# Expert rows built in two parts and a hand-written VectorE order between mixer and experts

## The chip, the cores and the metric

The kernel runs on one core of one Trainium2 chip. The time is device microseconds of one execution. Engines are named as in the profile: PE is TensorE, DVE is VectorE, ACT is ScalarE, POOL is GpSimd, SP is SyncE (it only issues transfers here).

## The reference

Two layers over 1024 tokens of width 1024, in float32. Layer 0 mixes with sliding-window attention, layer 1 with a diagonal state-space scan and a gated output projection (GLU). After each mixer comes a mixture of 32 experts:

```python
x = x + g1 * mix
h = rms_norm(x, norm_ffn[layer]) * (1.0 + sc2) + sh2
x = x + g2 * hierarchical_moe(h, ...)      # weights of this layer
```

The expert stage takes the softmax over 4 groups, the best group, and in it the two best of 8 experts. Each token goes to two experts, each `silu(x Wg) * (x Wu)` times `Wd` with 256 hidden columns, and the two results are added by their gates.

## The kernel before

Tokens stand in 8 row tiles of 128. Every float32 product is made of three products of a high and a low part; the low part of a weight tile comes from DVE (L939), the high part from ACT (L938). A layer runs in four steps: the mixer, its last projection, the handoff, and the experts.

The last projection runs in units. In layer 0 a unit is one row tile and one half of the columns (16 units, row by row). In layer 1 it is one row tile and a quarter of the columns (32 units, column by column, tile `x2`). Work of the routing is placed between the matmuls of a unit: `late(k)` takes the squares and transposes of unit k-1, and `early(k)` the logits of unit k-2. PE's order is the order of the code. DVE's order is chosen by a scheduler.

Once a row tile has all its logits, `scale` makes its `rms` by thirteen small dependent DVE operations (L720 to L118), and `rows_out` writes the expert row `h = (x * rms) * scr + shr` with two operations, L729 and L730, and sends it from POOL to `hrow` in DRAM. In layer 0 this is done in place in the residual's tile `xr`, which is also being stored to `xmid`. In layer 1 the row goes to a tile `hr` of two buffers.

Rows are routed in groups 0-2, 3-5 and 6-7 (`route`, tiles `r00`, `r03`, `r06` in layer 0 and `r10`, `r13`, `r16` in layer 1). A route finds the two experts of each token (L754 to L770), adds them to the running counts `seen` (L776), and lets PE make the positions within each expert (`lp`, L781/782, two `yield`s later). One step later the one-hot slots `so` (L803) let PE add the group to the lists in `lst` (L808). `drain` finishes what is left after the last unit.

`moe_lists` turns `lst` into the gather's indices `ligi` (L866, L867), the scatter's indices and gates, and `cnt` into the number of overflow blocks `nov`. `moe` then gathers rows for the first four experts into `xg` (L929), and PE transposes them (`e_0pt`, L949). Weight tiles come through the rotating tiles `w`, `pair` and `ring` on SP's queue. A load into a tile waits until the tile's last reader has ended, for a `w` tile often the low-part split L939. In layer 0 the experts run beside preparation for layer 1, which loads the tiles `b`.

## Time and profile before

| What | us |
|---|---|
| Median of 3 runs (lowest, highest) | 1846.93 (1841.4, 1850.45) |
| The profiled execution | 1847.04 |
| Its span, first to last instruction | 1845.3 |
| Output projection of layer 0, about | 366 to 500 |
| First handoff | 500 to 535 |
| Experts of layer 0 | 535 to about 880 |
| GLU projection of layer 1 | 1236 to 1438 |
| Second handoff | 1438 to 1473 |
| Experts of layer 1 | 1473 to 1800 |

Over the span PE is busy 84% and DVE 68%. Such shares are means over stages with different limits; what the change is worth is read in the two handoffs and in the units before them. A busy PE need not run at its full clock: the column PEclk gives the granted clock as a share of 2.4 GHz.

### The profile page before, as it was taken

How to read it: one execution, taken by the hardware profiler on the slowest of the kernel's cores; microseconds unless marked ns; L12 is line 12 of the kernel's file. 1: busy time of each engine (PE TensorE's matmuls, PEld its weight loads, DVE VectorE, ACT ScalarE, POOL GpSimd, SP SyncE). 2: the span in 40 equal slices, each digit the busy share in tenths (PEclk: the TensorE clock that was granted, in tenths of full speed). 3: DMA queues.
4: the chain of work that ended last, by engine and by line, in shares of the span. 5: the costliest groups of instructions: out<-in, count | busy, mean ns of one | idle time of the engine just before them, and what ended most of it. 6: DMA issues, size and time to landing. Idle time of an engine off the chain costs nothing. (4 is left out here: it accounts for less than half of the span.)

```text
span 1845.3 us, 20788 instructions
## 1 busy us (share of the span) xinstructions
PE 1559.1 (84%) x6935; PEld 1118.4 (61%) x6935; DVE 1247.4 (68%) x2311; ACT 748.9 (41%) x1455; POOL 438.2 (24%) x385
## 2 busy tenths in 40 slices
PE   4799969899849998999889677769999499999991
PEld 1576624377637665666467565648887377777760
DVE  4886779766567986766455699862216677777764
ACT  3211137621135554555311366532222165565640
POOL 1410014421112121111000577532220212222210
PEclk8799989999969999899999888889999599999995
DMA  9656750053449899989274011331002589999937
GB/s 364 216 212 245 294 151 1 15 206 120 172 164 355 303 330 327 318 324 318 94 257 149 25 37 40 97 124 46 33 18 88 214 320 348 381 388 374 360 124 281
DMA packets 124997, 379.85 MB, mean 206 GB/s; under 512 B 44908, under 2 KB 63428, under 8 KB 94168
## 3 DMA queue, kind: packets, MB, share of 16 engines
q1 hardware_dynamic: 94648, 301.89, 45.4%
q0 software_dynamic: 23040, 50.37, 7.2%
q10 hardware_dynamic: 7200, 26.22, 3.8%
q8 instruction: 57, 0.93, 0.2%
q14 instruction: 52, 0.43, 0.1%
HBM read 355.43 MB, written 56.53 MB: 223 GB/s over the span
## 5 line engine op out<-in xcount | busy, mean ns | idle before, releaser
L1742 PE MATMUL gpo<-gh,yh 128*128 128x512 f32 x256 | 106.7, 417 | 9.8 <-ACT gh L1717 9.8
L1742 PE MATMUL gpo<-gl,yh 128*128 128x512 f32 x256 | 101.5, 397 | 1.7 <-POOL gl L1718 1.7
L1742 PE MATMUL gpo<-gh,yl 128*128 128x512 f32 x256 | 101.4, 396 | 0.0
L929 POOL DMA_INDIRECT xg<-hrow,ligi x64 | 80.3, 1255 | 53.0 <-issue 14.9
L222 DVE SCALAR_TENSOR_TENSOR acc<-w,cs,acc 128x2048 f32<-128x2048 f32 x35 | 83.5, 2387 | 6.0 <-DMA w<-in_w_ada 5.6
L1748 DVE SCALAR_TENSOR_TENSOR gth<-gth,gpo 128x256 f32<-128x256 f32 x32 | 13.4, 419 | 107.4 <-ACT gth L1747 107.4
L1742 PEld LDWEIGHTS gpo<-gh,yh 128*128 128x128 f32 x256 | 49.2, 192 | 18.3 <-ACT gh L1717 10.1
L624 PE MATMUL wopo<-woh,a_hi 128*128 128x512 f32 x128 | 55.2, 431 | 1.6 <-ACT woh L598 1.6
L1742 PEld LDWEIGHTS gpo<-gl,yh 128*128 128x128 f32 x256 | 49.1, 192 | 10.5 <-POOL gl L1718 2.2
L1742 PEld LDWEIGHTS gpo<-gh,yl 128*128 128x128 f32 x256 | 48.8, 191 | 10.5
L624 PE MATMUL wopo<-wol,a_hi 128*128 128x512 f32 x128 | 52.7, 412 | 2.7 <-POOL wol L599 2.7
L1650 PE MATMUL bpo<-wih,bhh 128*128 128x512 f32 x128 | 52.0, 407 | 1.8 <-ACT bhh L1640 1.8
L624 PE MATMUL wopo<-woh,a_lo 128*128 128x512 f32 x128 | 52.3, 408 | 0.0
L1650 PE MATMUL bpo<-wil,bhh 128*128 128x512 f32 x128 | 50.9, 398 | 0.0
L1650 PE MATMUL bpo<-wih,bhl 128*128 128x512 f32 x128 | 50.1, 400 | 0.3 <-DVE bhl L1641 0.2
L1750 POOL TENSOR_TENSOR gth<-gth,g 128x256 f32<-128x256 f32 x24 | 17.5, 730 | 110.0 <-DVE gth L1748 110.0
L624 PEld LDWEIGHTS wopo<-wol,a_hi 128*128 128x128 f32 x128 | 25.4, 198 | 8.4 <-POOL wol L599 3.8
L1652 DVE SCALAR_TENSOR_TENSOR u<-bpo,n_y,shw 128x512 f32<-128x512 f32 x16 | 12.0, 750 | 26.4 <-PE bpo L1650 26.4
L1650 PEld LDWEIGHTS bpo<-wih,bhh 128*128 128x128 f32 x128 | 24.3, 190 | 8.9 <-ACT bhh L1640 3.7
L624 PEld LDWEIGHTS wopo<-woh,a_hi 128*128 128x128 f32 x128 | 25.1, 196 | 7.2 <-ACT woh L598 2.5
L624 PEld LDWEIGHTS wopo<-woh,a_lo 128*128 128x128 f32 x128 | 25.2, 197 | 6.0
L1650 PEld LDWEIGHTS bpo<-wih,bhl 128*128 128x128 f32 x128 | 24.2, 189 | 7.5 <-DVE bhl L1641 1.7
(2707 smaller groups left out, 4857.2 us busy)
## 6 DMA issues: line engine op xcount, KB each, us to landing
ring<-in_moe_w_down SPq DMA_DIRECT2D x64, 1024.0 KB
w<-in_w_ada SPq DMA_DIRECT2D x48, 1024.0 KB
w<-in_moe_w_gate SPq DMA_DIRECT2D x32, 1024.0 KB
w<-in_moe_w_up SPq DMA_DIRECT2D x32, 1024.0 KB
pair<-in_moe_w_gate SPq DMA_DIRECT2D x32, 1024.0 KB
pair<-in_moe_w_up SPq DMA_DIRECT2D x32, 1024.0 KB
w<-in_ssm_w_glu SPq DMA_DIRECT2D x16, 512.0 KB
w<-in_attn_w_qkv SPq DMA_DIRECT2D x6, 1024.0 KB
```

Of the source, the lines that this page charges most:

```text
L222: eng.scalar_tensor_tensor(acc, w, self.cs[:, j:j + 1], acc, op0=ALU.mult, op1=ALU.add)
L624: T.matmul(po, a[:, kk, j], w[:, j, :], start=(i == 0), stop=(i == 23))
L929: G.indirect_dma_start(out=self.xg, out_offset=None, in_=me.hrow[l], in_offset=bass.IndirectOffsetOnAxis(ap=self.gcol, axis=0), bounds_che ...
L1650: T.matmul(po, a[:, 4 * hf + j, :], w[:, j, :], start=(k == 0), stop=(k == 23))
L1652: V.scalar_tensor_tensor(u[:, 32 * c:32 * c + 32, 7 - i, :], po.rearrange("p (g c) -> p g c", c=16), r, self.shw[:, 512 * c:512 * c + 512] ...
L1742: T.matmul(po, a[:, 2 * q + j, :], w[:, j, :], start=(n == 0), stop=(n == 23))
L1748: V.scalar_tensor_tensor(th, th, 1.0, po[:, 0], op0=ALU.add, op1=ALU.mult)
L1750: E.tensor_tensor(th, th, g1[:, cs], op=ALU.mult)
```

## The change

An expert row is now made in two parts. `rows_in` makes `x * scr`, by halves in layer 0 and before `rms` is known, into a tile `hr` of its own (one buffer in layer 0, two in layer 1). `rows_out` makes `h * rms + shr` with one operation. In layer 0 the residual's tile `xr` has two buffers instead of three. Rows 6 and 7 are scaled one by one in both layers, the last row is written after its route, and `route` has one `yield` less. `drain` runs with DVE's order fixed as written, and `settle` advances the open routes. The weight splits of the first expert, the counts and `nov` are issued behind the copy `routed`. The pools of `moe` are opened in another order, so that `mw` (the split weight tiles) and the new `mx` (tiles `xh`, `xl`) lie elsewhere.

```diff
@@ mixer_a
-        units, early, late, drain = self.moe_front(0, 2, lambda nm: xp.tile([P, D], F32, name=nm, tag="xr", bufs=3))
+        units, early, late, settle, drain = self.moe_front(0, 2)
-                    xts[m] = xp.tile([P, D], F32, name=f"xr{m}", tag="xr", bufs=3)
+                    xts[m] = xp.tile([P, D], F32, name=f"xr{m}", tag="xr")
@@ moe_front
-        gain = rowtile(f"gain2{l}")
+        gain = fp.tile([P, D], F32, name=f"gain2{l}", tag="hr", bufs=1 + l)
...
+        def rows_in(m, lo, hi):
+            if m not in hs:
+                hs[m] = fp.tile([P, D], F32, name=f"f{l}{m}hr", tag="hr", bufs=1 + l)
+            V.tensor_tensor(hs[m][:, lo:hi], xs[m][:, lo:hi], scr[:, lo:hi], op=ALU.mult)
         def rows_out(m):
-            h = rowtile(f"f{l}{m}hr") if l else xs[m]
-            V.scalar_tensor_tensor(h, xs[m], rms[:, m:m + 1], scr, op0=ALU.mult, op1=ALU.mult)
-            V.tensor_tensor(h, h, shr, op=ALU.add)
+            if m not in hs:
+                rows_in(m, 0, D)
+            h = hs[m]
+            V.scalar_tensor_tensor(h, h, rms[:, m:m + 1], shr, op0=ALU.mult, op1=ALU.add)
             G.dma_start(hrows[:, m], h)
@@ route, before lp
             yield
-            yield
@@ route
-            S.activation(ex, ex, AF.Exp)
+            self.last_exp = S.activation(ex, ex, AF.Exp)
@@ late
                 hts[k - 1] = squares(m, xs[m], c)
+                if l == 0 or (c == parts - 1 and m >= GROUPS[-2]):
+                    rows_in(m, width * c, width * c + width)
+            if l and 0 <= k < len(units) and units[k][0] >= GROUPS[-2] and units[k][1] == parts - 1:
+                m = units[k][0]
+                xs[m] = tile_of(m)
+                rows_in(m, 0, D - width)
+        def finished(k):
+            if not 0 <= k < len(units):
+                return None
+            m, c = units[k]
+            logits(m, c, hts.pop(k))
+            if c < parts - 1 or m + 1 not in GROUPS:
+                if c == parts - 1 and (l == 0 or m >= GROUPS[-2]):
+                    scale(m, m + 1)
+                    rows_out(m)
+                return None
+            m0 = GROUPS[GROUPS.index(m + 1) - 1]
+            if l and m0 < GROUPS[-2]:
+                scale(m0, m + 1)
+                for i in range(m0, m + 1):
+                    rows_out(i)
+            else:
+                scale(m, m + 1)
+                if m + 1 < NT:
+                    rows_out(m)
+            return route(m0, m + 1)
         def early(k):
...
+            r = finished(k - 2)
+            settle()
+            if r:
+                next(r)
+                running.append(r)
+        def settle():
+            for r in list(running):
                 if next(r, True):
                     running.remove(r)
         def drain(tile_of):
             k = len(units)
-            early(k)
-            late(k, tile_of)
-            early(k + 1)
-            while running:
-                k += 1
-                early(k + 1)
+            with self.tc.manual_schedule(engines={ET.DVE}):
+                late(k, tile_of)
+                finished(k - 2)
+                settle()
+                last = finished(k - 1)
+                for _ in last:
+                    pass
+                rows_out(NT - 1)
@@ moe_lists (cnt's matmul now stands first)
         gi, si = self.index_cols(lp, self.lst[:, 0:NE], NE, "li")
-        V.tensor_copy(g, self.lst[:, NE:2 * NE])
+        self.routed = V.tensor_copy(g, self.lst[:, NE:2 * NE])
+        with self.tc.issue_after(self.routed.ins):
...
@@ moe
+        cm_x, xlp = self.open(f"mx{l}", 1)
         cm_rg, rgp = self.open(f"ring{l}", 1, side=("right", "left")[l])
...
+        cm_u, wp = self.open(f"mw{l}", 5)
         cm_m, mp = self.open(f"moe{l}", 2)
-        cm_u, wp = self.open(f"mw{l}", 5)
...
-        for q in range(4):
-            blocks[0].weights(q)
+        with tc.issue_after(self.routed.ins), tc.issue_after(self.last_exp.ins):
+            for q in range(4):
+                blocks[0].weights(q)
@@ mixer_b
+                if k == 31:
+                    settle()
```

Three places of the instruction orders follow. Names end in a number that tells copies of a tile apart. In the order after, lines from L730 on have moved down: L730 and L736 are the two parts of an expert row, L786/787 are `lp`, L808 is `so`, L813 is `lst`, L892 is `ligi`, L966 is the weight split and L770 of before is L776.

DVE at the end of the first handoff, before, from the first weight split to `ligi` (`e_0wl` is a low part of the first expert's weights, `cs` and `rem` are the counts):

```order
L939 TENSOR_TENSOR e_0wl_3945<-w_3931,e_0wh_3944 128x1024
L798 TENSOR_TENSOR r06tp<-r06lp,oh_2782 128x128
L939 TENSOR_TENSOR e_0wl_3949<-w_3931,e_0wh_3948 128x1024
L799 TENSOR_REDUCE pos<-r06tp 128x4
L882 COPY cs_3842<-cnt_3840 128x32
L803 TENSOR_TENSOR r06so<-slots,pos 128x256 x2
L886 TENSOR_SCALAR rem<-cs_3842 128x32
L939 TENSOR_TENSOR e_0wl_3953<-w_3931,e_0wh_3952 128x1024
L866 TENSOR_SCALAR lit<-lst_2779 128x32
L888 SCALAR_TENSOR_TENSOR rem<-cs_3842,rem 128x32
L939 TENSOR_TENSOR e_0wl_3957<-w_3931,e_0wh_3956 128x1024
L867 SCALAR_TENSOR_TENSOR ligi<-lst_2779,lit 128x32
```

The same place after (`f07hr` is the last expert row):

```order
L803 TENSOR_TENSOR r06tp<-r06lp,oh_2782 128x128
L804 TENSOR_REDUCE pos<-r06tp 128x4
L808 TENSOR_TENSOR r06so<-slots,pos 128x256 x2
L736 SCALAR_TENSOR_TENSOR f07hr<-f07hr,rms,shr 128x1024
L891 TENSOR_SCALAR lit<-lst_2779 128x32
L892 SCALAR_TENSOR_TENSOR ligi<-lst_2779,lit 128x32
L893 TENSOR_SCALAR lisi<-lst_2779 128x32
L905 COPY lgate_3851<-lst_2779 128x32
L908 COPY cs_3861<-cnt_3852 128x32
L911 MEMSET blk 128x32
L966 TENSOR_TENSOR e_0wl_3967<-w_3953,e_0wh_3966 128x1024
L912 TENSOR_SCALAR rem<-cs_3861 128x32
```

The four weight splits stood among the positions, slots and indices. Now the last row's second part stands there, and the splits come behind `lgate`, between the operations on the counts.

PE in the second last unit of the GLU stage, before (`gpo` are the projection's sums, `f143lg` the logits of row 4's last quarter, `r10lp` the positions of rows 0 to 2):

```order
L1742 MATMUL gpo_11084<-gh_10725,yh_9497 128x512
L1742 MATMUL gpo_11084<-gl_10726,yh_9497 128x512
L1742 MATMUL gpo_11084<-gh_10725,yl_9498 128x512
L709 MATMUL f143lg<-wr_9747,f143ht 128x128 x2
L781 MATMUL r10lp<-oh_9773,after 128x192
L782 MATMUL r10lp<-seen_9774,ones 128x192
```

PE one unit earlier, after (`f133lg` are the logits of row 3's last quarter):

```order
L1770 MATMUL gpo_11066<-gh_10748,yh_9518 128x512
L1770 MATMUL gpo_11066<-gl_10749,yh_9518 128x512
L1770 MATMUL gpo_11066<-gh_10748,yl_9519 128x512
L709 MATMUL f133lg<-wr_9770,f133ht 128x128 x2
L786 MATMUL r10lp<-oh_9796,after 128x192
L787 MATMUL r10lp<-seen_9797,ones 128x192
```

`r10lp` now follows the logits of row 3 instead of those of row 4, which is one unit of 24 matmuls earlier.

PE at the end of the second handoff, before (`f163lg` and `f173lg` are the last logits of rows 6 and 7):

```order
L709 MATMUL f163lg<-wr_9747,f163ht 128x128 x2
L701 MATMUL f173pt<-ident,x_9660 128x128 x2
L709 MATMUL f173lg<-wr_9747,f173ht 128x128 x2
L781 MATMUL r13lp<-oh_9773,after 128x192
L782 MATMUL r13lp<-seen_9774,ones 128x192
L808 MATMUL lst_9770<-rv_9776,r13so 128x128 x6
L781 MATMUL r16lp<-oh_9773,after 128x128
L782 MATMUL r16lp<-seen_9774,ones 128x128
L880 MATMUL cnt_11387<-seen_9774,ones 128x32
L808 MATMUL lst_9770<-rv_9776,r16so 128x128 x4
```

The same place after:

```order
L786 MATMUL r13lp<-oh_9796,after 128x192
L787 MATMUL r13lp<-seen_9797,ones 128x192
L701 MATMUL f173pt<-ident,x_9683 128x128 x2
L709 MATMUL f163lg<-wr_9770,f163ht 128x128 x2
L813 MATMUL lst_9793<-rv_9799,r13so 128x128 x6
L709 MATMUL f173lg<-wr_9770,f173ht 128x128 x2
L786 MATMUL r16lp<-oh_9796,after 128x128
L787 MATMUL r16lp<-seen_9797,ones 128x128
L903 MATMUL cnt_11426<-seen_9797,ones 128x32
L813 MATMUL lst_9793<-rv_9799,r16so 128x128 x4
```

`r13lp` has moved ahead of the last transposes, and `f173lg`, which the last route needs, has moved behind the `lst` matmuls of rows 3 to 5.

## Rows read from the trace of the kernel before

**Rows 1.** Five stages: us, busy us (instructions) per engine, PEclk, DMA share, GB/s.
```profile
366.00:500.00 134.00, 120.60 (x593) 98.02 (x594) 83.49 (x247) 27.29 (x57) 25.19 (x29) 0.96 0.44 160
500.00:535.00 35.00, 8.30 (x48) 6.94 (x46) 20.98 (x86) 6.46 (x10) 7.44 (x8) 0.62 0.50 177
535.00:880.00 345.00, 319.45 (x1294) 225.78 (x1295) 263.14 (x426) 186.86 (x264) 60.59 (x57) 0.97 0.88 315
...
1438.00:1473.00 35.00, 10.00 (x36) 7.83 (x36) 23.68 (x97) 6.06 (x11) 5.12 (x6) 0.53 0.59 213
1473.00:1800.00 327.00, 323.49 (x1339) 229.98 (x1340) 242.22 (x281) 187.96 (x252) 71.94 (x59) 0.99 0.85 328
```

**Rows 2.** Waits of PE, 378-505: us, times, longest.
```profile
PE f060pt L701 <- DVE xr L627: 3.7, 1, 3.7
PE r00lp L781 <- DVE lga L712: 2.7, 1, 2.7
...
PE r03lp L781 <- DVE lga L712: 1.1, 1, 1.1
```

**Rows 3.** Timeline of DVE, first handoff: start, length, operation, idle before.
```profile
502.56 0.16 DVE L720 TENSOR_REDUCE v<-vs 128x1 f32<-128x2 f32 x1 [0.41 <-ACT f071junk L697]
...
505.30 0.19 DVE L712 TENSOR_TENSOR lga<-lga,f071lg 128x36 f32<-128x36 f32 x1 [0.27 <-PE f071lg L709]
...
510.74 1.28 DVE L729 SCALAR_TENSOR_TENSOR xr<-xr,rms,scr 128x1024 f32<-128x1024 f32 x1 [4.78 <-DMA xmid<-xr]
511.94 0.15 DVE L754 TENSOR_REDUCE r06sm<-lga 128x2 f32<-128x8 f32 x1
...
524.95 0.18 DVE L867 SCALAR_TENSOR_TENSOR ligi<-lst,lit 128x32 int32<-128x32 f32 x1
```

**Rows 4.** Timeline of POOL, first handoff: the first gather.
```profile
525.97 1.54 POOL L929 DMA_INDIRECT xg<-hrow,ligi  x1 [11.86 <-DVE rem L888]
```

**Rows 5.** Timeline of PE, first handoff: first transposes of the experts.
```profile
535.27 1.12 PE L949 MATMUL e_0pt<-ident,xg 128*128 128x128 f32 x4 [11.71 <-DMA xg<-hrow,ligi]
```

**Rows 6.** Timeline of SP, first handoff: a weight load.
```profile
525.06 0.33 SPq L104 DMA_DIRECT2D w<-in_moe_w_gate  x1
```

**Rows 7.** Timeline of POOL, second handoff: the first gather.
```profile
1464.16 1.06 POOL L929 DMA_INDIRECT xg<-hrow,ligi  x1 [10.37 <-DVE nov L891]
```

**Rows 8.** Timeline of PE, end of layer 1's mixer and second handoff.
```profile
1411.67 0.61 PE L709 MATMUL f133lg<-wr,f133ht 128*128 128x128 f32 x4
...
1419.58 0.59 PE L781 MATMUL r10lp<-oh,after 128*128 128x192 f32 x2 [0.85 <-DVE lga L712]
...
1430.07 1.12 PE L808 MATMUL lst<-rv,r10so 128*128 128x128 f32 x4 [2.53 <-DVE r10so L803]
...
1445.83 3.24 PE L808 MATMUL lst<-rv,r13so 128*128 128x128 f32 x12 [3.59 <-DVE r13so L803]
...
1473.29 1.97 PE L949 MATMUL e_0pt<-ident,xg 128*128 128x128 f32 x8 [10.37 <-DMA xg<-hrow,ligi]
```

**Rows 9.** Gathers issued in 520-540, from issue to landing.
```profile
DMA to landing us min/median/max: 4.4/9.2/9.3
```

**Rows 10.** DMA issues in 1400-1475: two stores of expert rows, landing last.
```profile
hrow<-f12hr POOLq DMA_DIRECT2D x1, 512.0 KB, 2.9
...
hrow<-f17hr POOLq DMA_DIRECT2D x1, 512.0 KB, 5.4
```

**Rows 11.** Timeline of DVE, end of layer 1's mixer and second handoff.
```profile
1418.42 0.18 DVE L776 TENSOR_TENSOR seen<-seen,oh 128x32 f32<-128x32 f32 x1
...
1438.21 0.42 DVE L1751 TENSOR_TENSOR x<-x,gth 128x256 f32<-128x256 f32 x1
...
1440.69 1.22 DVE L939 TENSOR_TENSOR e_0wl<-w,e_0wh 128x1024 fp32r<-128x1024 f32 x1
...
1463.18 0.19 DVE L867 SCALAR_TENSOR_TENSOR ligi<-lst,lit 128x32 int32<-128x32 f32 x1
```

**Rows 12.** One stretch, 1427-1437, columns as in the first group.
```profile
1427.00:1437.00 10.00, 7.47 (x33) 6.12 (x32) 8.36 (x27) 1.33 (x5) 4.30 (x7) 0.83 0.39 158
```

More of the change, by code (lines that the diff above doesn't have):

```diff
@@ L821, in late @@
                 hts[k - 1] = squares(m, xs[m], c)
-        def early(k):
-            before = list(running)
-            if 0 <= k - 2 < len(units):
-                m, c = units[k - 2]
-                logits(m, c, hts.pop(k - 2))
-                if c == parts - 1:
-                    if l == 0:
-                        scale(m, m + 1)
-                    if m + 1 in GROUPS:
-                        m0 = GROUPS[GROUPS.index(m + 1) - 1]
-                        if l:
-                            scale(m0, m + 1)
-                        r = route(m0, m + 1)
-                        next(r)
-                        running.append(r)
-                    if l == 0:
-                        rows_out(m)
-                    elif m + 1 in GROUPS:
-                        for mm in range(m0, m + 1):
-                            rows_out(mm)
-            for r in before:
+                if l == 0 or (c == parts - 1 and m >= GROUPS[-2]):
[24 more added lines that the diff above has]
+            return route(m0, m + 1)
+        def early(k):
+            r = finished(k - 2)
[5 more added lines that the diff above has]
+            for r in list(running):
                 if next(r, True):
@@ L850, in drain @@
             k = len(units)
-            early(k)
-            late(k, tile_of)
-            early(k + 1)
-            while running:
-                k += 1
-                early(k + 1)
-        return units, early, late, drain
+            with self.tc.manual_schedule(engines={ET.DVE}):
[6 more added lines that the diff above has]
+                rows_out(NT - 1)
+        return units, early, late, settle, drain
     def index_cols(self, pool, src, n, nm):
@@ L875, in moe_lists @@
         g = lp.tile([P, NE], F32, name=f"lgate{l}", tag="lgate")
-        gi, si = self.index_cols(lp, self.lst[:, 0:NE], NE, "li")
-        V.tensor_copy(g, self.lst[:, NE:2 * NE])
         cnt = self.fpp.tile([P, 512], F32, name=f"cnt{l}", tag="lg")
         T.matmul(cnt[:, 0:NE], self.ones, self.seen[:, 2 * NT], start=True, stop=True)
-        cs = self.fp.tile([P, NE], F32, name=f"cs{l}", tag="cs")
-        V.tensor_copy(cs, cnt[:, 0:NE])
-        rem = self.save["rem"]
-        blk = self.save["blk"]
-        V.memset(blk, 1.0)
-        V.tensor_scalar(rem, cs, 128.5, None, op0=ALU.is_gt)
-        for k in range(2, 8):
-            V.scalar_tensor_tensor(rem, cs, 128.0 * k + 0.5, rem, op0=ALU.is_gt, op1=ALU.add)
-        nf = self.fp.tile([P, 1], F32, name=f"nf{l}", tag="nf")
-        V.tensor_reduce(nf, rem, AX.X, ALU.add)
-        V.tensor_copy(self.save["nov"], nf)
+        gi, si = self.index_cols(lp, self.lst[:, 0:NE], NE, "li")
+        self.routed = V.tensor_copy(g, self.lst[:, NE:2 * NE])
+        with self.tc.issue_after(self.routed.ins):
+            cs = self.fp.tile([P, NE], F32, name=f"cs{l}", tag="cs")
+            V.tensor_copy(cs, cnt[:, 0:NE])
+            rem = self.save["rem"]
+            blk = self.save["blk"]
+            V.memset(blk, 1.0)
+            V.tensor_scalar(rem, cs, 128.5, None, op0=ALU.is_gt)
+            for k in range(2, 8):
+                V.scalar_tensor_tensor(rem, cs, 128.0 * k + 0.5, rem, op0=ALU.is_gt, op1=ALU.add)
+            nf = self.fp.tile([P, 1], F32, name=f"nf{l}", tag="nf")
+            V.tensor_reduce(nf, rem, AX.X, ALU.add)
+            V.tensor_copy(self.save["nov"], nf)
         return gi, si, g
@@ L942, in transposes @@
             def transposes(self):
[L943 to L944 removed]
+                self.xh = xlp.tile([P, KT, P], F32R, name=self.nm + "xh", tag="xh", bufs=1)
+                self.xl = xlp.tile([P, KT, P], F32R, name=self.nm + "xl", tag="xl", bufs=1)
                 self.h = []
@@ L1727, in mixer_b @@
                 if k == 1:
-                    units, early, late, drain = self.moe_front(1, 4, lambda nm: self.fp.tile([P, D], F32, name=nm, tag="hr", bufs=2))
+                    units, early, late, settle, drain = self.moe_front(1, 4)
                 if i == 0 and 0 < c < 3:
```

8 lines of the change are left out of this document (3 added, 5 removed).

## The prediction

> **What bounds the kernel now.** I read the busy time by stage first [rows 1]. TensorE is nearly always busy in the two expert stages (319 of 345 us, 323 of 327) and in the output projection (121 of 134). It idles in the two handoffs: 8 of 35 us in 500-535 and 10 of 35 in 1438-1473. There the DMA share is 0.50 and 0.59 and VectorE is busy 21 and 24 us, so no engine is full: the handoffs are chains of waits, and the change is made in these chains. In the waits of TensorE the projection stage loses only a few us, 7.5 in the three largest [rows 2]. In the first handoff the timeline of VectorE shows what stands in the chain: the last row's write L729 waits 4.78 us for the store of `xmid`, and the routing of rows 6 and 7 (L754 on) is queued behind it [rows 3]. The gather starts at 525.97 [rows 4], 1.0 us behind the start of L867. It lands only when e_0pt can start, 9.3 us later [rows 5], and a weight load was issued at 525.06, right before it [rows 6]. The second handoff has the same end: gather at 1464.16 [rows 7], e_0pt at 1473.29, 9.1 us later [rows 8]. Of the gathers issued around the first handoff one landed in 4.4 us while the median took 9.2 [rows 9]. So about half of the landing is other traffic.
>
> **The change, part by part.** The sum is made against the profiled execution, 1847.04 us (span 1845.3); the median shown is 1846.93, so the difference can be put on either.
>
> *Projection stage, layer 0.* A row write was L729 and L730 in place, some 2.5 us once the scale is known. Now the product with `scr` is made by halves before that, and one operation of 1.28 [rows 3] is left. It no longer waits for the `xmid` store, which gives up to 4.8. Against this, the position matmul (r00lp, r03lp) stands one unit earlier in TensorE's order. A unit is 120.6/16 = 7.5 us [rows 1]. Before, r00lp came two units behind the logits and still waited 2.7, so VectorE needed 15.1 + 2.7 = 17.8 for this stretch. Less 1.2 and 4.8 it needs 11.8, which is 4.3 more than one unit: the wait grows by 1.6. For r03lp (1.1 before) the same sum gives 2.7, again 1.6 more. The wait of f060pt, 3.7, goes. That is -0.5, and I take -1 with the small waits. Two new waits stand here. The first half of the next row waits for the store of the row before to land, since layer 0 has one such buffer. Behind it on VectorE wait the two operations that empty PSUM, which four PSUM buffers cover for three units. The load of row m+2 waits for the `xmid` store of row m, and the stores of expert rows are queued behind it on POOL. A store landed in 2.9 here, the last one, with loads beside it, in 5.4 [rows 10], less than a unit. Bounds of the stage: -8 (all of [rows 2] goes and the rest with it) and +6 (both position matmuls wait a unit).
>
> *First handoff.* L712 of the last logits started at 505.30. The twelve matmuls of r03 no longer stand in front of f071pt; at the lower clock (0.53 granted in 1438-1473 [rows 1]) twelve of them took 3.24 [rows 8], and I take 0.9 of it as gained: 504.4. The scale is now behind L712: 2.5 (502.56 to 505.30 less 0.27 of waiting) and then 0.66 less L712's 0.2 for the last two operations before the routing [rows 3]. L754 follows at 507.5 instead of 511.94. From L754 to L867 it was 13.0; a row operation of 1.2 and four weight splits of 1.22 [rows 11] leave. Part of them had covered waits for TensorE and dependent small operations, so I take 2.7 of these 6.1 as gained: L867 at 517.8 instead of 524.95. That is not the gather's start. The last row is now written behind the last L803, issued at about 517 and landed 3.5 to 4 later, and the gather waits for it: 521.0, a gain of 5.0. The splits now come behind the routing, four of them in 5 us, and the next weight load waits for the fourth, so it is issued near 523 and the gather goes ahead of it. I take 4.4 for the landing [rows 9] and 0.5 because the gather beside a split took 1.54 and the one beside an idle VectorE 1.06 [rows 4, 7]: 4.9 instead of 9.3. e_0pt comes at 525.9, 9.4 earlier. Bounds: -5 (landing as before) and -11. With the stage before it: -10.4. MoE 0 passes it on, I think, since its loads are issued as TensorE and VectorE free the buffers; its own idle 26 us [rows 1] stay.
>
> *One rule bears on those splits.* The row shows 0.48 us for a gather beside a split. The Trainium skill (SBUF — State Buffer, "Who interferes with whom") says that a VectorE instruction with two inputs in SBUF contends with a GpSimd instruction that reads SBUF, and the one that came second is blocked until the first has ended. By it each of the new splits beside the gather can hold it for its whole length, so 0.7 more than I take in each handoff, and the sum would be 1.4 higher; the trace has one such pair and shows the smaller figure.
>
> *End of the GLU stage, layer 1.* r10lp also moves one unit up, behind f133lg, which ends near 1412.3 [rows 8]. The last `seen` is ready at 1418.6 [rows 11]; VectorE has about the same work in front of it as before. TensorE stands 6.3 us. The idle of 2.53 before lst [rows 8] was followed by a mean clock of 0.83 over ten us [rows 12], that is 3.4 us at the lower of the two levels and 1.7 lost; I take 2.3 for the longer stop. What goes: 0.85, 2.53 [rows 8] and that 1.7. Net 6.3 + 2.3 - 5.1 = +3.5. Bounds +1 and +7.
>
> *Second handoff.* From L1751 (1438.21) to L867 (1463.18) it was 25.0 [rows 11]. Five splits (5.8) and four row operations (4.8) leave: -10.6. In come the two operations for row 5 that are left (2.4), the product for row 7 (1.3) and one for row 6 (1.2): +4.9. A second scale chain for the last row alone, as in [rows 3]: +3.0. r13lp, before hidden beside other work: +1.6. f173lg, now queued behind the twelve lst matmuls of r13 (3.24 [rows 8]): +3.3. In the hand-written order some fifty small operations, which had run between others at about 0.1 us each, follow one another at about 0.19, as the scale chain does: +4.5. So L867 comes 6.7 later. The store of row 7 again ends the chain, 1.6 behind that: the gather starts 8.3 later. With the landing at 4.9 instead of 9.1, e_0pt comes 4.1 later. Bounds -1 (small operations hidden) and +8.5 (landing as before). MoE 1 passes it on in full: TensorE is busy 323 of 327 us [rows 1]. The hand order also puts the chain that ends in `nov` before the low part of the first block's inputs. That ends about 8 us behind L867, when e_0pt is just done: nothing, or 1 us.
>
> *The rest.* Moving the tile pools and the earlier `cnt` matmul cost nothing: neither is waited for by what ends the chain.
>
> Sum: -10.4 + 3.5 + 4.1 = -2.8, so 1844.2; I say **1844 us**.
>
> **Rivals.** (a) *The projection stage gains in full.* If VectorE reaches the end of each route within a unit, the waits of [rows 2] go and layer 0 gives -8 - 9.9; with +6 for layer 1 that is -12, 1835. For it speaks the wait of 4.78 on a store, which also delayed rows before the last. Against it: 17.8 us is far from 7.5.
> (b) *Weights late: slower.* The loads behind the splits now start after the routing. Between 1438 and 1473 the DMA moved 213 GB/s for 35 us, 7.5 MB [rows 1]; now about 2 MB go before e_0pt. The 5.5 MB at 328 GB/s are 16 us of lead. If the stream has no slack, TensorE waits for weights within the first experts and the whole lead is paid: 1844 + 14 to 16, so 1859. It decides once the weights of the third or fourth expert land after TensorE has asked for them. Against it: the share was 0.85 during MoE 1 with TensorE full.
> (c) *The landing is the gather's own.* Then 9.2 us stay and both handoffs lose 4.3: 1853. One gather of 4.4 speaks against it.
> (d) *The tiles laid clear free nothing*, because the order puts the splits behind the routing anyway. Then the splits come where the order says, as I have summed; the time is the forecast's.
>
> **How the numbers follow.** The forecast with (d) 0.38, (a) 0.27, (b) 0.20, (c) 0.15. A difference under 0.5%, 9.2 us, cannot be told from none here, so "same" is 1837.7 to 1856.2. The forecast's own range is 1836 to 1852: a twentieth of the total goes to faster from it. Faster 0.32, same 0.48, slower 0.20. The range 1831 to 1859 takes in (a) and (c) and reaches to (b).
>
> **What would show it.** In the profile after: TensorE waiting 5 to 7 us for r10lp behind f133lg, and some us for r00lp and r03lp; no wait of a row write on the `xmid` store; L866/L867 in the first handoff about 7 us sooner, and the gather then waiting for the store of row 7; gathers that land in about 5 us in both handoffs; f173lg behind the lst matmuls of r13, and the second gather some 8 us later measured from L1751. Wrong I would be if the gathers still take 9 us, if TensorE waits for weights in the first experts, or if the first handoff ends as late as before.

## The result, and the profile after

| | Median us (lowest, highest) | Runs |
|---|---|---|
| Before | 1845.45 (1841.40, 1850.45) | 20 |
| After | 1853.26 (1848.13, 1861.55) | 20 |

The ratio is 1.0051, with a 95% interval of 1.0037 to 1.0065: slower by about 8 to 9 us, where 1844 and a small gain had been forecast. Of the 20 runs after, 14 lie at 1848 to 1856 and six at 1860 to 1862; the 20 of before show no such second group. The profiled execution after took 1852.55, with a span of 1850.6. Line numbers below are those of the kernel after: L730 and L736 are the two parts of an expert row, L786/787 `lp`, L808 `so`, L892 `ligi`, L956 the gather, L966 the weight split, L976 `e_pt`, L1781 the last addition to `x`. The versions of the experiments shift them by up to ten lines.

To compare executions that start a stage at different times I use the distance between two marks.

| From, to (us) | Before | After | Forecast of the difference | Measured |
|---|---|---|---|---|
| First to last `wopo` (projection, layer 0) | 133.6 | 136.3 | -1 | +2.7 |
| Last `wopo` to `e_0pt` | 35.4 | 27.0 | -9.4 | -8.4 |
| `e_0pt` to `e_31pt`, layer 0 | 347.2 | 345.2 | 0 | -2.0 |
| `e_31pt` to first `gpo` | 343.9 | 348.3 | 0 | +4.4 |
| First to last `gpo` (GLU, layer 1) | 210.0 | 213.1 | +3.5 | +3.1 |
| Last `gpo` to `e_0pt`, layer 1 | 36.9 | 46.1 | +4.1 | +9.2 |
| `e_0pt` to `e_31pt`, layer 1 | 308.6 | 308.2 | 0 | -0.4 |

The fourth row lies outside the change. Over all runs of this study it took 343 to 348 without a pattern, so I count it as spread between executions. Two stages went wrong, the first and the sixth: 3.7 and 5.1 us above their forecasts, together about the 8 us between the forecast and the profiled execution.

The stages of after, to be read against [rows 1]; columns are the stretch, its length, busy us (instructions) of PE, PEld, DVE, ACT and POOL, PEclk, DMA share, GB/s:

```profile
366.00:500.00 134.00, 121.23 (x596) 99.96 (x597) 85.04 (x256) 25.60 (x55) 22.15 (x26) 0.92 0.44 155
...
1437.00:1481.00 44.00, 11.38 (x40) 9.16 (x40) 30.91 (x122) 6.24 (x11) 9.84 (x10) 0.53 0.28 104
1481.00:1790.00 309.00, 307.79 (x1291) 221.47 (x1292) 236.96 (x273) 185.70 (x248) 69.89 (x57) 0.99 0.93 357
```

In the projection the clock fell from 0.96 to 0.92. In the second handoff the DMA share halved, from 0.59 to 0.28. In the experts of layer 1 TensorE is full (307.8 of 309 us): rival (b), weights that come late there, did not happen.

The waits of TensorE in the projection (compare [rows 2]), in us, times, longest:

```profile
PE r03lp L786 <- DVE lga L714: 7.9, 1, 7.9
PE r00lp L786 <- DVE lga L714: 3.0, 1, 3.0
```

`f060pt` has gone from the list, as forecast; `r03lp` waits 7.9 where 2.7 was forecast (`r00lp` 3.0 where 4.3 was). The timeline of VectorE (and one row of PE) shows what stood in front of it: start, length, operation, idle before.

```profile
465.71 1.28 DVE L736 SCALAR_TENSOR_TENSOR f05hr<-f05hr,rms,shr 128x1024 f32<-128x1024 f32 x1
...
478.86 0.69 DVE L730 TENSOR_TENSOR f06hr<-xr,scr 128x512 f32<-128x512 f32 x1 [7.13 <-DMA hrow<-f05hr]
479.46 0.16 DVE L766 TENSOR_TENSOR r03t<-desc,r03sm 128x12 f32<-128x12 f32 x1
...
484.57 0.24 DVE L776 TENSOR_TENSOR oh<-desc,r03mi 128x96 f32<-128x96 f32 x1
...
484.98 1.01 PE L786 MATMUL r03lp<-oh,after 128*128 128x192 f32 x2 [7.94 <-DVE lga L714]
```

The first half product of row 6 waits 7.13 for the store of row 5 to leave the only buffer `hr`, and the rest of the route r03, on which `r03lp` rests, is queued behind it.

That wait is longer than a store. Row 5 was finished at 466.99, and the buffer was free again 11.9 us later. POOL shows why:

```profile
462.65 0.53 POOL L629 DMA_DIRECT2D xmid<-xr  x1 [8.46 <-DVE xr L627]
472.96 0.53 POOL L612 DMA_DIRECT2D xr<-in_x  x1 [9.77 <-DMA xmid<-xr]
473.48 0.53 POOL L737 DMA_DIRECT2D hrow<-f05hr  x1
```

The load of row 7 into `xr`, which now has two buffers, waits until the `xmid` store of row 5 has landed, 10.3 us after its issue. The store of the expert row stands behind that load in POOL's order and goes out 6.5 us late; 5.4 us later `hr` is free. In the kernel before, the row write itself waited for the same `xmid` store, and the route r03 was behind it too, but TensorE came to `r03lp` only at 493.6 (DVE, then PE, of before):

```profile
476.83 1.28 DVE L729 SCALAR_TENSOR_TENSOR xr<-xr,rms,scr 128x1024 f32<-128x1024 f32 x1 [6.98 <-DMA xmid<-xr]
```

```profile
494.72 0.59 PE L781 MATMUL r03lp<-oh,after 128*128 128x192 f32 x2 [1.15 <-DVE lga L712]
```

In the kernel after it came there at 477.0.

The first handoff came out nearly as forecast (compare [rows 4 to 6]); POOL, PE, SP and DVE:

```profile
519.33 0.53 POOL L737 DMA_DIRECT2D hrow<-f07hr  x1 [4.74 <-DVE f07hr L736]
523.98 1.07 POOL L956 DMA_INDIRECT xg<-hrow,ligi  x1 [4.11 <-DMA hrow<-f07hr]
...
528.44 1.97 PE L976 MATMUL e_0pt<-ident,xg 128*128 128x128 f32 x8 [8.80 <-DMA xg<-hrow,ligi]
...
525.26 0.33 SPq L104 DMA_DIRECT2D w<-in_moe_w_gate  x1
...
524.01 1.23 DVE L966 TENSOR_TENSOR e_0wl<-w,e_0wh 128x1024 fp32r<-128x1024 f32 x1
```

The gather waits for the last row's store and starts 4.65 behind its issue; it goes ahead of the weight load and lands in 4.5. It was ahead of the fourth split by only 0.03 us, and e5 below shows what follows when it is not.

The second handoff has the same order of work and another end (compare [rows 7, 8, 11]); DVE, POOL, SP and PE:

```profile
1437.10 0.42 DVE L1781 TENSOR_TENSOR x<-x,gth 128x256 f32<-128x256 f32 x1
...
1467.49 0.19 DVE L892 SCALAR_TENSOR_TENSOR ligi<-lst,lit 128x32 int32<-128x32 f32 x1
...
1471.60 1.22 DVE L966 TENSOR_TENSOR e_0wl<-w,e_0wh 128x1024 fp32r<-128x1024 f32 x1
1472.83 1.22 DVE L966 TENSOR_TENSOR e_1wl<-w,e_1wh 128x1024 fp32r<-128x1024 f32 x1
...
1466.92 0.53 POOL L737 DMA_DIRECT2D hrow<-f17hr  x1 [15.91 <-DVE f17hr L736]
1472.01 3.02 POOL L956 DMA_INDIRECT xg<-hrow,ligi  x1 [4.55 <-DVE rem L914]
...
1472.84 0.33 SPq L104 DMA_DIRECT2D w<-in_moe_w_gate  x1
...
1481.09 1.97 PE L976 MATMUL e_0pt<-ident,xg 128*128 128x128 f32 x8 [13.87 <-DMA xg<-hrow,ligi]
```

`ligi` comes 30.4 behind L1781 (25.0 before). The gather starts 4.5 later still, 5.1 behind the issue of the store that it waits for, and it arrives 0.41 us behind the start of a split. It takes 3.02 instead of 1.07 and ends at 1475.03, 0.98 behind the end of the second split. By then the weight load of 1472.84 is out. The landing takes 9.1 from the gather's start, as before.

### The profile page after: what moved, and what is told of

Read it like the earlier page. It is cut to its first block, busy times and chain, and to the rows that moved or that the text cites. A ratio compares the mean times of both kernels' runs of the same rounds, so it can differ in the third digit from the quotient of the medians.

```text
span 1850.6 us, 20822 instructions
## 1 busy us (share of the span) xinstructions
PE 1559.9 (84%) x6935; PEld 1120.2 (61%) x6935; DVE 1255.6 (68%) x2336; ACT 748.9 (40%) x1455; POOL 441.7 (24%) x385
## 5 line engine op out<-in xcount | busy, mean ns | idle before, releaser
L956 POOL DMA_INDIRECT xg<-hrow,ligi x64 | 83.6, 1307 | 32.1 <-issue 14.9
```

The source lines that it names most:

```text
L956: G.indirect_dma_start(out=self.xg, out_offset=None, in_=me.hrow[l], in_offset=bass.IndirectOffsetOnAxis(ap=self.gcol, axis=0), bounds_che ...
```

## The experiments

Every time is a median of 5 to 12 runs, beside runs of the kernel before on the same chip; a ratio is to before. The median of before was 1845.5 to 1848.6 on these chips, so between chips a ratio says more than a difference of medians. Unless another kernel is named, an edit is made to the kernel after, whose ratio is 1.0051 (1.0037, 1.0065). Stage lengths come from one profiled execution each; that was the fastest of the runs for e6 (1835.77), the slowest for e10 (1867.63) and the slowest but one for e5 (1854.88).

| Run | Median us | Ratio (95%) |
|---|---|---|
| e1 both positions a unit back | 1837.72 | 0.9956 (0.9936, 0.9977) |
| e5 only layer 0 | 1850.08 | 1.0020 (1.0005, 1.0036) |
| e6 only layer 1 | 1844.70 | 0.9995 (0.9975, 1.0015) |
| e13 row product later | 1843.16 | 0.9964 (0.9947, 0.9982) |
| e2 split with one SBUF input | 1850.34 | 1.0023 (1.0004, 1.0041) |
| e3 last row early | 1848.13 | 1.0010 (0.9997, 1.0023) |
| e4 splits free | 1859.19 | 1.0075 (1.0051, 1.0100) |
| e11 scheduler's order | 1840.65 | 0.9970 (0.9954, 0.9986) |
| e7 = e1 + e3 | 1834.87 | 0.9933 (0.9909, 0.9957) |
| e8 = e7 + last logits first | 1832.82 | 0.9927 (0.9899, 0.9956) |
| e9 = e8 + two splits free | 1833.14 | 0.9934 (0.9913, 0.9956) |
| e10 pools as before | 1860.57 | 1.0077 (1.0057, 1.0096) |
| e12 = e1 + e11 | 1824.73 | 0.9896 (0.9879, 0.9914) |
| e14 = e12 + e13 | 1815.91 | 0.9840 (0.9824, 0.9857) |

### Waits in the projections: e1, e5, e6, e13

e1 puts the second `yield` back where before had cover for it, and lets the drain run the routes out:

```diff
             yield
+            if l == 0 or m0 == 0:
+                yield
...
-                settle()
+                while running:
+                    settle()
```

> The changed kernel with the position matmuls r00lp, r03lp (layer 0) and r10lp (layer 1) one unit later again, as before the change; all else stays. Theory A (these three matmuls, which come before VectorE has ended the route, cost the gain of the projection stages): in the changed kernel they waited 3.0, 7.9 and 4.9 us, and the clock was low after each. Without them the output projection ends 9 to 11 us sooner and the GLU stage 3 to 4: about 1841 us, 11 to 14 below the changed kernel. Rival B (the single buffer for expert rows and the slower order of VectorE hold the stage anyway, and TensorE only waits at another place): the stage gains under 4, about 1850. Rival C (the loss is in the second handoff): no difference in the stages, 1853.

1837.72: the position matmul was worth more than the whole loss. First to last `wopo` took 129.0 (after 136.3), the GLU stage 206.2 (after 213.1). e5 and e6 split the edit, with `if l == 0:` and `if l and m0 == 0:`.

> The position matmuls of layer 0 (r00lp, r03lp) go back one unit; layer 1 stays as in the changed kernel. Theory A (a position matmul that stands too early on TensorE costs the wait and the lower clock behind it): the two waits of 3.0 and 7.9 us go to about 2 and 1, the first handoff ends about 6 us earlier than after (e_0pt near 522.5), and about 5 of it reach the end: 1848. Rival B (the wait only moves idle time that TensorE has to spend anyway, the store of the expert rows setting the pace): e_0pt near 528 and 1853. What is left of the 15 us of the run with both restored is then layer 1's share.

> Only r10lp of layer 1 goes back one unit; layer 0 stays as in the changed kernel. Theory A: r10lp's wait of 4.9 us goes, the GLU stage ends 3.5 to 5 earlier, and nothing before it moves: e_0pt of layer 0 at 528.4, total 1853 - 9 = 1844 if the two layers add up to the 15 us of the run with both (9 to 10 here, some of it because the last logits stand on another place of the drain when the routes are run through to their end). Rival B (layer 1's handoff is set by VectorE's chain behind the last unit, so an earlier end of TensorE is waited away): the x add earlier by 4, e_0pt of layer 1 by less than 1 from it, total 1852.

Layer 0 alone gives 0.3%, layer 1 alone 0.6%. e6 met its number. e5 came out between its two theories: its stage is short (128.4), but its first handoff took 34.5. There the first gather started level with a split and took 3.50, where e1's took 1.07 (rows of both in the last section); e_0pt came at 530.0 and not at 522.5. The code of layer 0 is the same in e1 and e5, so this difference is one between executions.

In e1, too, VectorE stood 7.38 us for the buffer `hr`; the later position matmul only kept TensorE from standing with it. e13 takes that wait away and leaves the position where the change put it:

```diff
-                if l == 0 or (c == parts - 1 and m >= GROUPS[-2]):
+                if l == 0 and c == parts - 1:
+                    rows_in(m, 0, D)
+                if l and c == parts - 1 and m >= GROUPS[-2]:
                     rows_in(m, width * c, width * c + width)
```

> The changed kernel, but in layer 0 the product with scr is made in one piece after the second half of the row, one unit later; all else as changed. Theory A (r03lp's 7.9 us come from the product of row 6 that waits 7.13 for the one buffer hr, with the route queued behind it on VectorE): the store of row 5 has landed by then or VectorE waits for it only behind the route, r03lp waits 1 to 3, the projection stage (first to last wopo) takes 130 to 132 instead of 136.3, total 1853 - 5 = 1848 (1846 to 1850). Rival B (the position matmul one unit earlier is too early for VectorE whatever the buffer does): r03lp still waits 6 to 8, stage 135 to 137, total 1853.

Theory A, and by more than it said. VectorE and PE of e13:

```profile
475.75 1.23 DVE L730 TENSOR_TENSOR f06hr<-xr,scr 128x1024 f32<-128x1024 f32 x1 [0.98 <-DMA hrow<-f05hr]
...
474.65 0.59 PE L786 MATMUL r03lp<-oh,after 128*128 128x192 f32 x2 [0.60 <-DVE lga L714]
```

The wait for the buffer is 0.98 and lies behind the route; `r03lp` waits 0.60. First to last `wopo` takes 122.8, 13.5 less than after. `r00lp` waits 0.6 instead of 3.0, and the granted clock of 425 to 440 is 1.00 instead of 0.77. The median moved by 10, the ratio by 0.9%: layer 0's early position is harmless once nothing stands in front of the route. The loss there needs both, the wait in front of the route and the early matmul behind it: e5 takes away the second and comes to 128.4, e13 the first and comes to 122.8, and with both gone (e14) it is 122.5. That `xr` has two buffers, which puts the load and with it the store late, was not tried by itself.

### The landing in the second handoff: e2, e3, e4

e2 lets the first expert's splits subtract a tile of zeros in PSUM, so that each has one input in SBUF. It leaves out the true low part of that expert's weights, so its result is not the reference's:

```diff
-                V.tensor_tensor(lo, r, hi.bitcast(F32), op=ALU.subtract)
+                V.tensor_tensor(lo, r, zero[:, None].to_broadcast([P, 2, 2, 256]), op=ALU.subtract)
```

> The changed kernel, in which the four low-part splits of the first expert of each layer subtract a zero tile in PSUM and not the high part in SBUF; so the low part of that expert is not computed. Each split then has one input in SBUF. Theory A (a split with two inputs in SBUF keeps GpSimd from making the gather's and the last store's transfers): in the changed kernel the first gather of the second handoff took 3.02 us on GpSimd and ended 0.99 us after the last split. Here it takes about 1.0, only the first split of the second expert can still hold one gather, and the store of the last row lands in some 3 us where it took 4.6 and 5.1; e_0pt comes 2 to 5 us sooner behind the ligi operation in the second handoff and 1 to 2 in the first: 1847 to 1850. Rival B (the weight loads, which are issued just then, delay the gather): the gather still takes 2 to 3 us on GpSimd or its landing stays 9, and the time stays within 1 us of 1853.

POOL and PE of e2 in the second handoff:

```profile
1463.28 0.53 POOL L737 DMA_DIRECT2D hrow<-f17hr  x1 [15.89 <-DVE f17hr L736]
1468.22 1.06 POOL L956 DMA_INDIRECT xg<-hrow,ligi  x1 [4.41 <-DVE rem L914]
...
1472.68 1.97 PE L979 MATMUL e_0pt<-ident,xg 128*128 128x128 f32 x8 [9.10 <-DMA xg<-hrow,ligi]
```

The store is about as slow as after (4.9 from its issue to the gather's start, 5.1 after), but the gather takes 1.06 in the midst of the splits and has landed 4.5 behind its start, not 9.1. So the second SBUF input of the split is what held the gather. Last `gpo` to `e_0pt` fell by 3.9 to 42.2; the median fell by only 2.9, since the experts of layer 1 took 313.8 instead of 308.2. The intervals of e2 and of after still touch.

e3 writes the last row ahead of its route:

```diff
                 last = finished(k - 1)
+                rows_out(NT - 1)
                 for _ in last:
                     pass
-                rows_out(NT - 1)
```

> The changed kernel with the last row's second part and its store ahead of the last route and not behind it, in both layers. Theory A (the landing of this store, 4.1 and 4.5 us after the last index, sets the gather): the index comes 1.2 us later, but the gather can start 1.0 behind it, so it starts 2 us sooner in the first handoff and 2.4 in the second; there splits may then hold it until they end, so that less is left. 1848 to 1851. Rival B (the gather waits for something else, the splits): it starts or ends no sooner, and the 1.2 us of the row write are lost in each handoff: 1855.

The store was out at 1454.93, `ligi` came at 1464.53 and the gather 0.98 later, ahead of the second split; it took 1.59 and had landed 4.8 behind its start. The row's 1.3 us now stand in front of the route, and `ligi` is 31.4 behind L1781 instead of 30.4; the handoff took 39.3. The median fell by 5, the ratio by 0.4%.

e4 frees the splits from the routing:

```diff
-        with tc.issue_after(self.routed.ins), tc.issue_after(self.last_exp.ins):
-            for q in range(4):
-                blocks[0].weights(q)
+        for q in range(4):
+            blocks[0].weights(q)
```

> The changed kernel without the rule that puts the weight splits of the first expert behind the routing: the scheduler then puts them among the operations of rows 3 to 5 and ahead of the last route, where they were before; the weight loads that wait for them are issued sooner too. Theory A (splits beside the gather, and loads that go out with it, cost the second handoff its landing): the first gather of the second handoff takes 1.0 on GpSimd and lands in 4 to 5 us instead of 9.1, against 3 to 4 us of splits on the chain: 4 to 6 us sooner in the second handoff, and no change or 1 to 2 us slower in the first: 1848 to 1851. Rival B (the chain on VectorE is what costs): each split on the chain costs its 1.2 us, so 5 us slower in the second handoff and 3 in the first, with 4 gained by the gather: 1855 or more.

Rival B: the splits stood in the chain. `ligi` came 34.6 behind the last addition, and 1859.19 is the slowest but one. The gather, which now met no split, took 1.06 and still landed 8.7 behind its start, where theory A had 4 to 5. POOL, SP and PE of e4:

```profile
1480.25 1.06 POOL L956 DMA_INDIRECT xg<-hrow,ligi  x1 [4.48 <-DMA hrow<-f17hr]
...
1479.19 0.81 SPq L104 DMA_DIRECT2D ring<-in_moe_w_down  x2
...
1488.97 1.97 PE L976 MATMUL e_0pt<-ident,xg 128*128 128x128 f32 x8 [13.42 <-DMA xg<-hrow,ligi]
```

Weight loads were out before the gather ended. That is the pattern of all 16 profiled executions, two handoffs each: in the 20 where SP issued no load in the 9 us before the first gather or until it ended, it had landed 4.3 to 4.9 behind its start; in the other 12 it took 7.0 to 10.8, held or not. So the hold cost the landing by letting the loads go first. What the loads do to the gather on its way no run shows. Holding the splits behind the routing was right; the intervals of e4 and of after overlap, so this rests on the handoffs (50.8 against 46.1, and 32.0 against 27.0). What was wrong is the last row's store, which let the gather come after the splits.

### The order of the drain: e11

```diff
-            with self.tc.manual_schedule(engines={ET.DVE}):
+            if True:
```

> The changed kernel with the drain's VectorE order left to the scheduler. Theory A (the hand order makes some fifty small operations follow one another, 0.19 each instead of 0.1): ligi in layer 1 comes 30.4 - 4.5 = 26 us behind the last x add, total 1853 - 4 to 5 = 1848. Rival B (the small operations depend on one another in any order, or the scheduler puts row operations of 1.2 us among them): ligi at 30 to 33 behind the x add, total 1853 to 1856.

Theory A in the chain (`ligi` 25.7 behind L1781), and a gain of 12.6 where 4 to 5 was expected. Much of the rest is the gather (the second handoff takes 34.5 instead of 46.1): the scheduler writes the last row right behind its scale, so that POOL issues the store at 1450.44 and nothing waits for it.

```profile
1459.60 0.19 DVE L892 SCALAR_TENSOR_TENSOR ligi<-lst,lit 128x32 int32<-128x32 f32 x1
...
1450.44 0.53 POOL L737 DMA_DIRECT2D hrow<-f17hr  x1 [8.68 <-DVE r16sm L760]
1460.57 1.59 POOL L956 DMA_INDIRECT xg<-hrow,ligi  x1 [9.60 <-DVE blk L911]
...
1465.47 1.97 PE L976 MATMUL e_0pt<-ident,xg 128*128 128x128 f32 x8 [6.13 <-DMA xg<-hrow,ligi]
```

### What a shorter handoff runs into: e7, e8, e9

e7 joins the edits of e1 and e3; e8 also puts the last logits ahead of the `lst` matmuls:

```diff
                 finished(k - 2)
+                last = finished(k - 1)
                 while running:
                     settle()
-                last = finished(k - 1)
```

> Both position matmuls go back one unit and the last expert row is written ahead of its route. Theory: the two gains are in different places (end of the projection; store and gather) and add: against the changed kernel 15.5 + 5 = 20, so 1833 (1830 to 1836), with gathers of 1.5 us that start within 1.2 us of ligi, landed in 4.7. Rival: the gain of the early last row was already had by the restored yield (ligi is then what ends last, and the row's 1.3 us stand in front of it on VectorE): same as the run with the yield alone, 1838.

> As the run with both changes, and the last logits (f071lg, f173lg) and their scale stand ahead of the lst matmuls of the group before. Theory: TensorE no longer makes the last logits wait for twelve lst matmuls (2.96 us) and the r13so that they need; in layer 1 ligi comes 3 us sooner, in layer 0 less than 1: 1830. Rival: VectorE is the chain, and the scale of the last row (2.5 us) now only stands ahead of the slots r13so instead of behind: 0, so the time of the other run within 2 us.

e7's gain over e1 is 2.9 by the medians of two jobs, with intervals that overlap. Its second handoff is 7.0 shorter than e1's (38.5 against 45.5), but its experts of layer 1 take 314.5 instead of 306.9. The waits of TensorE there, in e7, and ACT's row:

```profile
PE e_1ph L1006 <- DVE e_1hid L1000: 4.6, 1, 4.6
```

```profile
1477.41 3.90 ACT L968 ACTIVATE e_2wh<-pair 128x1024 fp32r<-128x1024 f32 x4 [7.81 <-DMA pair<-in_moe_w_up]
1481.21 0.36 ACT L999 ACTIVATE e_1hid<-e_1gu 128x256 f32<-128x256 f32 x1
```

ACT stands 7.81 for a weight tile of expert 2, the activation of expert 1 is queued behind it, and TensorE waits. This is rival (b) in a small form, which was hidden as long as the gather was late. e8 shortened the handoff to 36.3 and the time by 2.0, which its interval does not separate from e7. e9 frees two of the four splits of e8, so that weight loads start earlier:

```diff
+        for q in range(2):
+            blocks[0].weights(q)
         with tc.issue_after(self.routed.ins), tc.issue_after(self.last_exp.ins):
-            for q in range(4):
+            for q in range(2, 4):
                 blocks[0].weights(q)
```

> As the run with the last logits first, but two of the four weight splits of the first expert no longer wait for the routing. There the second handoff took 37 us from the last gpo to e_0pt, yet the experts of layer 1 took 313 us from e_0pt to e_31pt instead of 308, because TensorE waits 4.6 for e_1hid, which stands on ACT behind a weight tile that lands late. Theory A (the weight loads start too late, since SP's queue is in order and the next w load waits for a split): the loads start 5 us or more earlier, the wait of TensorE goes, e_0pt to e_31pt 308 to 309; the two splits lengthen the chain by up to 2.4, so 1830 (1828 to 1833). Rival B (the loads behind w wait for tiles of the mixer, not for the split, as the ring load before the change did until 1460): 313 stays and the splits cost 2.4: 1835.

TensorE's wait for `e_1ph` fell from 3.7 (e8) to 2.7, and the time is e8's. What the loads gave, the splits on VectorE took: in the profiled executions the experts of layer 1 are 2.0 shorter than in e8 (311.6 against 313.6) and the handoff is 2.2 longer (38.5).

### The pools: e10

```diff
-        cm_u, wp = self.open(f"mw{l}", 5)
         cm_m, mp = self.open(f"moe{l}", 2)
+        cm_u, wp = self.open(f"mw{l}", 5)
```

(and `xh`, `xl` back in `moe`, without the pool `mx`)

> The changed kernel with the pools of the expert stage opened as before (split weight tiles and xh, xl where they were). Theory A (the relaid tiles free nothing, since the order puts the splits behind the routing anyway): 1853 within 2, e_0pt of both layers at 27 and 46 us behind the last projection matmul as after. Rival B (without the move the high parts on ACT and the splits wait for the scratch of the front end): the splits of the first expert come later, e_0pt unchanged but the experts wait for weights, 3 to 6 slower: 1857.

Slower than after by 0.26% (about 5 us), though the two intervals overlap a little. The mechanism of rival B is not what the trace shows: the first split starts 0.44 us behind `ligi` in the first handoff (523.70 to 524.14), as it does after. POOL clears the tiles `xg` with memsets, and in e10 four of them fall into the end of the GLU stage, where they hold a small operation of route r13 on VectorE:

```profile
1444.83 3.65 POOL L941 MEMSET xg<- 128x1024 f32 x4
```

```profile
1445.36 3.15 DVE L767 TENSOR_SCALAR r13t<-r13t 128x12 f32<-128x12 f32 x1
```

The same operation took 0.17 elsewhere. `r13lp` waits 9.5 instead of 6.6. In the first handoff of e10 the gather lost against the splits as in e5 (3.50). Which share of the 5 us is the first, and which the second, is open.

### The parts that lose, taken out: e12, e14

e12 has the edits of e1 and e11, e14 that of e13 as well.

> The changed kernel with both position matmuls back one unit and the drain's VectorE order left to the scheduler; of the change remain the rows in two parts, the moved pools and the splits behind the routing. Theory A (the two losses are in different places: the waits in front of and within the projections, and the chain behind the last unit): against the changed kernel 15 + 12 = 27 less what the experts of layer 1 give back for starting earlier (up to 5): 1826 to 1831. Rival B (with the earlier position matmul undone the drain had already lost most of its length, so the scheduler has little left to hide): 1836 to 1838, as the run with the positions alone.

> The version with both position matmuls back and the scheduler's order, with the product of layer 0 one unit later as well. Theory A: with the position matmul two units behind the logits TensorE waits 0.9 for r03lp and 4.1 for the transposes f061pt behind an x update that stands behind the buffer wait; the 4.1 goes: 1825 - 3 = 1822. Rival B (a full row's product of 1.2 us behind the second half only moves the wait to the last row, where it is on the chain): 1825 to 1827.

e12: 1824.73, so the losses of position and of order add up. e14: 1815.91, a ratio of 0.9840 to before. The stage of e14 took 122.5 and not e12's 126.6, which is the 4.1 of `f061pt`; the first handoff is the same (23.0, e12 22.7). The other 5 of the 9 us between the two lie in other stages and are not explained. Two stages of e14, to be read against [rows 1], columns as there:

```profile
366.00:485.80 119.80, 116.85 (x590) 97.05 (x590) 81.66 (x248) 24.13 (x53) 19.93 (x24) 0.97 0.49 171
485.80:508.40 22.60, 8.24 (x47) 6.99 (x47) 18.73 (x71) 6.47 (x10) 9.01 (x9) 0.72 0.47 157
```

TensorE is busy 117 of 120 us in the projection, and the handoff is 23 us instead of 35.

## Why the prediction was wrong

**Projection stage: the step that failed first.** The text named the wait for the one buffer `hr` and then said: "Behind it on VectorE wait the two operations that empty PSUM". The route of the group before was queued there too. And it priced the wait by a store's landing, 2.9 to 5.4, "less than a unit"; the row was ready 11.9 us before its buffer was free, since its store stood on POOL behind a load that waited for `xmid`. In the trace of before it was the `xmid` store that the row write waited for [rows 3]; I counted that wait as gone, up to 4.8. It had only changed its name: 6.98 for `xmid` at row 5 before, 7.13 for `hrow` at row 6 after, both in front of the rest of the route, and now with TensorE nearer behind it. The forecast was -1, measured +2.7, and e13 shows that without the wait it would have been -11. That is rival (a) in size, and it was there to be had.

**First handoff: right, with luck.** Forecast -9.4, measured -8.4, with the late store, the gather ahead of the weight load and a landing of 4.5 as described. But the text had the gather 2 us ahead of that load, and it was ahead of the fourth split by 0.03; in e5, where it was not, the handoff took 34.5 and the landing 10.5.

**GLU stage: right.** Forecast +3.5, measured +3.1; `r10lp` waits 4.9 (forecast 5 to 7). e6 took it away again.

**Second handoff: the step that failed second.** The forecast was a `ligi` 6.7 later (measured 5.4, although the sum left out the last row's second part, 1.3, which also stands ahead of `ligi`) and a gather 8.3 later (9.0, both measured from the last addition to `x`), which was nearly right; and a landing of 4.9, where it took 9.1. That landing is 4.2 of the 5.1 us. "I take 4.4 for the landing and 0.5 because the gather beside a split took 1.54" failed: 0.5 was the price of the end of one split, and this gather met two. It took 3.02, a weight load was issued before it ended, and with that the landing was the long one; in e4 a gather behind such loads landed in 8.7 without any hold. The Trainium skill (SBUF — State Buffer, "Who interferes with whom") says that the one of the two engines that comes second is blocked until the other's instruction has ended. The trace agrees: with one input of the split in PSUM (e2) the hold was gone, which is the page's condition. Here the gather did not get in between the first split and the second either; in e3 and e11 it did, at the end of the first, and took 1.59. I had weighed that rule at 0.7 per handoff, and took less.

**The chain of small operations: right.** +4.5 had been put on the hand-written order; the scheduler's order gave back 4.7 of `ligi` (30.4 to 25.7). From the last addition to `ligi` one small operation follows the other after 0.16 us before, 0.20 after and 0.17 in e11. The early store came with the scheduler's order and was not in that sum, so that e11's second handoff is 11.6 shorter than after's.

**Rivals.** (b), late weights, did not happen in the changed kernel, and in the form of 2.7 to 4.6 us of waiting it takes its share of every shorter second handoff (e2, e3, e7 to e9, e11, e12, e14). (c) fell: in the first handoff and in e2 the gather landed in 4.5. That the median, 1853.26, is its 1853 is chance: the long landing stayed in one handoff, in which loads went ahead of the gather, and the rest came from the projection. (d) holds for the splits, which start as early behind `ligi` in e10; what the pools changed there is when POOL clears `xg`.

## What to carry to other kernels

A buffer that is filled early moves a wait; it does not remove it. Before counting such a wait as gone, look for the store that must leave the buffer, for what stands in front of that store in its engine's order, and for everything that stands behind the early write. Where a transfer is started by GpSimd beside VectorE operations with two SBUF inputs, what matters is whether it comes ahead of them and of the next loads, or behind; here that decided 4 us in the second handoff (e2) and 6 in the first (e1 against e5). And when a chain gets shorter, the next thing on the path (the weight loads here) takes its part of the gain.

## What the runs showed of the hardware that was not expected

- The hold between VectorE and GpSimd runs both ways. A gather beside splits took 1.54, 2.01, 3.02 and up to 3.50, alone 0.99 to 1.07, beside splits with a PSUM input 1.02 to 1.07 (e2); a VectorE operation of 0.17 took 3.15 beside a memset on POOL (e10).
- Who comes first is a matter of hundredths. In after, e1, e5, e6, e10 and e13 the first gather of layer 0 met the fourth split; POOL and DVE of e1, then of e5 and of e10:

```profile
518.31 1.07 POOL L959 DMA_INDIRECT xg<-hrow,ligi  x1 [4.14 <-DVE e_0wl L969]
...
518.32 1.25 DVE L969 TENSOR_TENSOR e_0wl<-w,e_0wh 128x1024 fp32r<-128x1024 f32 x1
```

```profile
519.54 3.50 POOL L959 DMA_INDIRECT xg<-hrow,ligi  x1 [4.15 <-DVE e_0wl L969]
...
519.54 1.22 DVE L969 TENSOR_TENSOR e_0wl<-w,e_0wh 128x1024 fp32r<-128x1024 f32 x1
```

```profile
527.80 3.50 POOL L955 DMA_INDIRECT xg<-hrow,ligi  x1 [4.14 <-DVE e_0wl L965]
...
527.80 1.22 DVE L965 TENSOR_TENSOR e_0wl<-w,e_0wh 128x1024 fp32r<-128x1024 f32 x1
```

In e1 the gather started 0.01 us ahead and took 1.07, as it did in after, e6 and e13, 0.01 to 0.03 ahead; in e5 and e10 it started at the same reading, and took 3.50. The handoff was 28.4 in e1 and 34.5 in e5. I think, without having shown it, that this is part of the spread of the kernel after (13 us over 20 runs, against 9 over 20 of before), and that the six runs at 1860 to 1862 are those in which the gather came second.
- The 7.9 us that TensorE stood for `r03lp` cost somewhat more than 7.9. Between 480 and 502 the granted clock was 0.77 (0.92 before), and a lead of 9.6 us on before at the logits of row 6's first half had become a lag of 2.0 at those of the second half. Of these 11.6 us 7.9 are the wait, 2.0 the `r03lp` matmuls, which before stood behind those logits, and 1.7 the slower matmuls right behind them.
